# Taking the last two reciprocals of a layer normalisation on GpSimd, as powers of -1, instead of on VectorE

## Chip, cores, metric

One core of one Trainium2 chip. The metric is device time in microseconds (us) of one execution; a run's verdict is "same" when the ratio lies within 2%. Kernels are compared only within the same rounds.

## The reference

```python
# x: float32 [32, 512, 1024], eps = 1e-5
mean = np.mean(x, axis=-1, keepdims=True)
var = np.var(x, axis=-1, keepdims=True)
return ((x - mean) / np.sqrt(var + eps)).astype(np.float32)
```

16384 rows of 1024 values: 67.1 MB in and 67.1 MB out.

## The kernel before

Rows are taken in groups of 128 (one per partition). A tile is eight groups (4 MB); the last two tiles, numbers 15 and 16, have six and two. A ring of six slots in SBUF holds the tiles, and the outputs overwrite the inputs in place. Per tile: SyncE loads; VectorE computes statistics of each half row; GpSimd combines the halves into the negated mean and the sum of squares; ScalarE takes the root; VectorE the reciprocal; GpSimd the product -mean/std; ScalarE writes the normalised rows and issues the store.

```python
TILES = (8,) * 15 + (6, 2)
# ... VectorE, per tile t of K groups that starts in slot `at`
    for k in range(K):
        for s in range(NSUB):
            i = nc.vector.bn_stats(out=stats[:, at + k, s, :], in_=...)   # first one waits for landed[t]
    i.then_inc(taken, 1)
    nc.vector.reciprocal(
        out=rstd[:, at : at + K], in_=std[:, at : at + K]
    )._wait_ge(rooted[t], turn).then_inc(inverse, 1)
# ... GpSimd, per tile: nine small instructions from `taken` to ss, then
    ready.append(gp(g.tensor_mul(out=nmr[...], in0=nm, in1=rstd[...]), inverse, t + 1))
# ... ScalarE, per tile
    nc.scalar.activation(out=std[...], in_=ss[...], func=AF.Sqrt, ...)._wait_ge(*summed[t]).then_inc(rooted[t], 1)
    for k in range(at, at + K):          # the first one waits for ready[t]
        nc.scalar.activation(out=ring[:, k, :], in_=ring[:, k, :], func=AF.Identity,
                             bias=nmr[:, k : k + 1], scale=rstd[:, k : k + 1]).then_inc(act, 1)
    nc.scalar.dma_start(out=<rows of out>, in_=ring[...])._wait_ge(act, ...).then_inc(stored[t], 16)
```

Of the kernel before, what the change touches and what calls it, by code (L numbers as in the profile page):

```python
# [11 lines left out]
SLOT, SLOTS = 8, 6  # L12

FIRST, TURNS = 3, 2

HALVES, PARTS = (4, 4), (8,)

# [2 lines left out]
def kernel(  # L20
# [6 lines left out]
    nc = tc.nc  # L27
    P = nc.NUM_PARTITIONS
# [12 lines left out]
    ALU = mybir.AluOpType  # L41

    def sbuf(name, shape):
        return ctx.enter_context(nc.sbuf_tensor(name, shape, fdt))


    plan, row = [], 0
    for K in TILES:
# [10 lines left out]
    ss, nmean, std, rstd, nmr = (  # L59
        sbuf(n, [P, SLOT * SLOTS]) for n in ("ss", "nmean", "std", "rstd", "nmr")  # L60
    )
    eps_t = sbuf("eps_t", [P, 1])




    def places(name):
        out = [nc.alloc_semaphore(f"{name}_{t}") for t in range(FIRST + SLOTS)]
        for t in range(len(out), len(plan)):
            looped = t < FIRST + TURNS * SLOTS  # L70
            out.append(out[t - SLOTS] if looped else nc.alloc_semaphore(f"{name}_{t}"))
        return out

    def sixteens(sems, t):
# [4 lines left out]
    landed, rooted, stored = places("landed"), places("rooted"), places("stored")  # L79
    taken, inverse, pool, act = map(  # L80
        nc.alloc_semaphore, ("taken", "inverse", "pool", "act")
    )

    def rows_of(a, row, K):
        return a[row * P : (row + K) * P].rearrange("(p k) d -> p k d", p=P)
# [3 lines left out]
    K, row, at = plan[0]  # L89
    first = 0  # L90
    for n, engine, sem in zip(HALVES, (nc.sync, nc.scalar), (landed[0], later)):
        engine.dma_start(
            out=ring[:, at + first : at + first + n, :],
# [5 lines left out]
    for t, (K, row, at) in list(enumerate(plan))[1:]:  # L99
        gone = sorted({owner[r] for r in range(at, at + K) if r in owner})  # L100
        owner.update((r, t) for r in range(at, at + K))
        for g in gone[:-1]:
            nc.sync.wait_ge(stored[g], sixteens(stored, g))
        dma = nc.sync.dma_start(
            out=ring[:, at : at + K, :], in_=rows_of(x2, row, K)
# [5 lines left out]
    def vector(t, arrived, turn):  # L111
        K, row, at = plan[t]
        for k in range(K):
            for s in range(NSUB):
                i = nc.vector.bn_stats(  # L115
                    out=stats[:, at + k, s, :],
                    in_=ring[:, at + k, s * BN_MAX : (s + 1) * BN_MAX],
                )
                if k == 0 and s == 0:
                    i._wait_ge(landed[t], arrived)  # L120
                if t == 0 and k == HALVES[0] and s == 0:
                    i._wait_ge(later, 16)
        i.then_inc(taken, 1)
        nc.vector.reciprocal(  # L124
            out=rstd[:, at : at + K], in_=std[:, at : at + K]
        )._wait_ge(rooted[t], turn).then_inc(inverse, 1)

    nc.vector.memset(eps_t[:], eps_val)  # L128
    for t in range(FIRST):
        vector(t, 16, 1)  # L130
    turn = nc.vector.alloc_register("turn")
# [2 lines left out]
    with nc.vector.Fori(16, 16 * TURNS + 1, 16) as arrived:  # L134
        for t in range(FIRST, FIRST + SLOTS):
            vector(t, nc.vector.lower_val(arrived), turn)
        nc.vector.reg_add(turn, turn, 1)
    for t in range(FIRST + TURNS * SLOTS, len(plan)):
        vector(t, 16, 1)
# [4 lines left out]
    def gp(i, sem, value):  # L144
        nonlocal npool
        i._wait_ge(sem, value).then_inc(pool, 1)
        npool += 1
        return pool, npool

    g = nc.gpsimd  # L150
    for t, (K, row, at) in enumerate(plan):
        parts = stats[:, at : at + K].rearrange("p g s (h c) -> p g (s h) c", h=2)
        mean4, m2 = parts[:, :, :, 1], parts[:, :, :, 2]
        nm, d, h = nmean[:, at : at + K], dev[:, :K], half[:, :K]
        n = gp(
            g.tensor_tensor(out=h, in0=mean4[:, :, 0:2], in1=mean4[:, :, 2:4], op=ALU.add),  # L156
            taken,
            t + 1,
        )
        n = gp(g.tensor_tensor(out=nm, in0=h[:, :, 0], in1=h[:, :, 1], op=ALU.add), *n)  # L160
        n = gp(
            g.tensor_scalar(out=nm, in0=nm, scalar1=-1.0 / H, scalar2=None, op0=ALU.mult),  # L162
            *n,
        )
        n = gp(
            g.tensor_tensor(  # L166
                out=d, in0=mean4, in1=nm.unsqueeze(2).to_broadcast([P, K, H]), op=ALU.add
            ),
            *n,
        )  # L170
        n = gp(g.tensor_mul(out=d, in0=d, in1=d), *n)  # L171
        n = gp(
            g.tensor_scalar(  # L173
                out=d, in0=d, scalar1=float(D // H), scalar2=None, op0=ALU.mult
            ),
            *n,
        )
        n = gp(g.tensor_tensor(out=d, in0=d, in1=m2, op=ALU.add), *n)  # L178
        n = gp(g.tensor_tensor(out=h, in0=d[:, :, 0:2], in1=d[:, :, 2:4], op=ALU.add), *n)  # L179
        summed.append(  # L180
            gp(
                g.tensor_tensor(  # L182
                    out=ss[:, at : at + K], in0=h[:, :, 0], in1=h[:, :, 1], op=ALU.add
                ),
                *n,
            )
        )
        ready.append(
            gp(
                g.tensor_mul(  # L190
                    out=nmr[:, at : at + K], in0=nm, in1=rstd[:, at : at + K]
                ),
                inverse,
                t + 1,
            )
        )


    for t, (K, row, at) in enumerate(plan):
        nc.scalar.activation(  # L200
            out=std[:, at : at + K],
# [7 lines left out]
        for k in range(at, at + K):  # L209
            i = nc.scalar.activation(  # L210
                out=ring[:, k, :],
# [7 lines left out]
            if k - at + 1 in ends:  # L219
                n = parts[ends.index(k - at + 1)]  # L220
                a = k + 1 - n
                nc.scalar.dma_start(
                    out=rows_of(o2, row, K)[:, a - at : a - at + n, :], in_=ring[:, a : a + n, :]
# [41 lines left out]
```

## Time and profile before

| | before |
|---|---|
| time, median of 3 runs | 317.83 us (317.74 to 318.22) |
| span of the profile | 315.9 us |
| VectorE, ScalarE, GpSimd busy | 156.8, 153.0, 39.3 us |
| DMA | 134.24 MB, 425 GB/s over the span |
| issue of the last two stores | 294.43 and 298.01 us |
| landing of the last two stores | 312.2 and 314.7 us |

The upper rows say that no compute engine is the bound. More than 16 us pass between the last instruction of any compute engine and the last byte on the ground.

### The profile page before, as it was taken

The numbers are of one execution on the slowest core, as the hardware profiler recorded it, in microseconds if no ns is written. First come the engines' busy times: TensorE is split into PE (matmuls) and PEld (weight loads), VectorE is DVE, ScalarE is ACT, GpSimd is POOL, SyncE is SP. The second block draws the span as 40 slices with busy tenths as digits, with TensorE's granted clock in tenths as the row PEclk, the third lists the DMA queues.
The fourth block names the chain that finished last, engine by engine and source line by source line (L and its number), as shares of the span: only waits on it lengthen the run. The fifth ranks groups of instructions, "written<-read, shape, count | busy, mean of one in ns | idle before, by whom it ended". The sixth has DMA issues, their size and how long they took to land.

```text
span 315.9 us, 694 instructions
## 1 busy us (share of the span) xinstructions
DVE 156.8 (50%) x274; ACT 153.0 (48%) x146; POOL 39.3 (12%) x174
## 2 busy tenths in 40 slices
DVE  0296595965190752908438093470925619193000
ACT  1006595865925609165190742908338092476600
POOL 0002202022002020020201102011020200203100
DMA  7999999999999999999999999999999999999996
GB/s 292 438 452 411 452 402 407 457 407 461 403 462 415 448 419 444 419 444 431 431 436 427 444 423 440 423 448 415 452 415 456 419 431 442 435 430 427 427 421 288
DMA packets 5043, 134.24 MB, mean 425 GB/s; under 512 B 560, under 2 KB 560, under 8 KB 560
## 3 DMA queue, kind: packets, MB, share of 16 engines
q10 hardware_dynamic: 2592, 69.21, 51.0%
q1 hardware_dynamic: 2448, 65.01, 47.9%
q14 instruction: 3, 0.02, 0.0%
HBM read 67.11 MB, written 67.11 MB: 425 GB/s over the span
## 4 chain that ended last, share of the span: by engine, by line
DMA 61%; DVE 18%; ACT 9%; POOL 4%; issue 2%; ACTq 0%; DVEq 0%; SPq 0%
DMA ring<-in_x_dram 31%; DMA out_dram<-ring 29%; DVE stats L115 17%; ACT ring L210 9%; ACT std L200 1%; POOL dev L173 1%; POOL dev L178 1%; POOL dev L166 0%; POOL dev L171 0%; POOL nmean L162 0%; POOL half L156 0%; POOL half L179 0%; POOL ss L182 0%; DVE rstd L124 0%; POOL nmean L160 0%
## 5 line engine op out<-in xcount | busy, mean ns | idle before, releaser
L115 DVE BATCH_NORM_STATS2 stats<-ring 128x6 f32<-128x512 f32 x256 | 153.5, 678 | 82.2 <-DMA ring<-in_x_dram 81.6
L210 ACT ACTIVATE ring<-ring,nmr,rstd 128x1024 f32<-128x1024 f32 x128 | 146.6, 1227 | 9.3 <-POOL nmr L190 9.3
L200 ACT ACTIVATE std<-ss,eps_t 128x8 f32<-128x8 f32 (+2 forms) x17 | 5.1, 300 | 134.3 <-POOL ss L182 133.9
L156 POOL TENSOR_TENSOR half<-stats 128x16 f32<-128x16 f32 (+2 forms) x17 | 3.9, 232 | 232.9 <-DVE stats L115 232.9
L124 DVE RECIPROCAL rstd<-std 128x8 f32<-128x8 f32 (+2 forms) x17 | 3.4, 200 | 55.4 <-ACT std L200 55.4
L173 POOL TENSOR_SCALAR dev<-dev 128x32 f32<-128x32 f32 (+2 forms) x17 | 5.0, 293 | 1.5
L190 POOL TENSOR_TENSOR nmr<-nmean,rstd 128x8 f32<-128x8 f32 (+2 forms) x17 | 3.5, 203 | 11.9 <-DVE rstd L124 11.9
L178 POOL TENSOR_TENSOR dev<-dev,stats 128x32 f32<-128x32 f32 (+2 forms) x17 | 4.3, 254 | 1.4
L166 POOL TENSOR_TENSOR dev<-stats,nmean 128x32 f32<-128x32 f32 (+2 forms) x17 | 4.1, 239 | 1.4
L171 POOL TENSOR_TENSOR dev<-dev 128x32 f32<-128x32 f32 (+2 forms) x17 | 4.0, 235 | 1.3
L162 POOL TENSOR_SCALAR nmean<-nmean 128x8 f32<-128x8 f32 (+2 forms) x17 | 4.0, 233 | 1.5
L179 POOL TENSOR_TENSOR half<-dev 128x16 f32<-128x16 f32 (+2 forms) x17 | 3.6, 213 | 1.3
L182 POOL TENSOR_TENSOR ss<-half 128x8 f32<-128x8 f32 (+2 forms) x17 | 3.4, 201 | 1.3
L160 POOL TENSOR_TENSOR nmean<-half 128x8 f32<-128x8 f32 (+2 forms) x17 | 3.4, 200 | 1.3
L200 ACT ACT_TABLE_LOAD x1 | 1.3, 1283 | 1.3 <-SPq L52 1.3
L128 DVE MEMSET eps_t<- 128x1 f32 x1 | 0.1, 59 | 1.0 <-SPq L52 1.0
L246 POOL MEMSET const-float32-0.0<- 128x1 f32 x1 | 0.1, 98 | 0.2 <-issue 0.2
L246 POOL MEMSET const-uint8-127<- 128x1 uint8 x1 | 0.1, 102 | 0.0
L246 POOL MEMSET const-bfloat16-1.0<- 128x1 bf16 x1 | 0.1, 101 | 0.0
L246 POOL MEMSET const-float32-1.0<- 128x1 f32 x1 | 0.1, 98 | 0.0
## 6 DMA issues: line engine op xcount, KB each, us to landing
out_dram<-ring ACTq DMA_DIRECT2D x15, 4096.0 KB, 47.4
ring<-in_x_dram SPq DMA_DIRECT2D x14, 4096.0 KB, 44.3
ring<-in_x_dram SPq DMA_DIRECT2D x1, 3072.0 KB, 42.0
out_dram<-ring ACTq DMA_DIRECT2D x1, 3072.0 KB, 17.8
ring<-in_x_dram ACTq DMA_DIRECT2D x1, 2048.0 KB, 12.4
ring<-in_x_dram SPq DMA_DIRECT2D x1, 2048.0 KB, 12.5
ring<-in_x_dram SPq DMA_DIRECT2D x1, 1024.0 KB, 53.7
out_dram<-ring ACTq DMA_DIRECT2D x1, 1024.0 KB, 16.7
```

Source lines behind the costliest of these rows:

```text
L115: i = nc.vector.bn_stats(out=stats[:, at + k, s, :], in_=ring[:, at + k, s * BN_MAX : (s + 1) * BN_MAX],)
L124: nc.vector.reciprocal(out=rstd[:, at : at + K], in_=std[:, at : at + K])._wait_ge(rooted[t], turn).then_inc(inverse, 1)
L156: g.tensor_tensor(out=h, in0=mean4[:, :, 0:2], in1=mean4[:, :, 2:4], op=ALU.add),
L162: g.tensor_scalar(out=nm, in0=nm, scalar1=-1.0 / H, scalar2=None, op0=ALU.mult),
L166: g.tensor_tensor(out=d, in0=mean4, in1=nm.unsqueeze(2).to_broadcast([P, K, H]), op=ALU.add),
L171: n = gp(g.tensor_mul(out=d, in0=d, in1=d), *n)
L173: g.tensor_scalar(out=d, in0=d, scalar1=float(D // H), scalar2=None, op0=ALU.mult),
L178: n = gp(g.tensor_tensor(out=d, in0=d, in1=m2, op=ALU.add), *n)
L179: n = gp(g.tensor_tensor(out=h, in0=d[:, :, 0:2], in1=d[:, :, 2:4], op=ALU.add), *n)
L190: g.tensor_mul(out=nmr[:, at : at + K], in0=nm, in1=rstd[:, at : at + K]),
L200: nc.scalar.activation(out=std[:, at : at + K], in_=ss[:, at : at + K], func=AF.Sqrt, bias=eps_t[:], scale=1.0 / D,)._wait_ge(*summed[t]). ...
L210: i = nc.scalar.activation(out=ring[:, k, :], in_=ring[:, k, :], func=AF.Identity, bias=nmr[:, k : k + 1], scale=rstd[:, k : k + 1],).then ...
```

## The change

Intent: VectorE's end takes two instructions fewer. In the last two tiles GpSimd takes std to the power of -1 itself; its product then waits for its own power instead of for VectorE.

```diff
+LAST = 2
...
+    power = sbuf("power", [P, SLOT])
...
         i.then_inc(taken, 1)
+        if t >= len(plan) - LAST:
+            return
         nc.vector.reciprocal(
...
     nc.vector.memset(eps_t[:], eps_val)
+    nc.vector.memset(power[:], -1.0)
...
+        if t < len(plan) - LAST:
+            n = inverse, t + 1
+        else:
+            n = gp(
+                g.tensor_tensor(out=rstd[:, at : at + K], in0=std[:, at : at + K],
+                                in1=power[:, :K], op=ALU.pow),
+                rooted[t],
+                1,
+            )
         ready.append(
             gp(
                 g.tensor_mul(
                     out=nmr[:, at : at + K], in0=nm, in1=rstd[:, at : at + K]
                 ),
-                inverse,
-                t + 1,
+                *n,
             )
         )
```

More of the change, by code (lines that the diff above doesn't have):

```diff
@@ L187 @@
         )
+        if t < len(plan) - LAST:
+            n = inverse, t + 1
+        else:
+            n = gp(
+                g.tensor_tensor(
+                    out=rstd[:, at : at + K],
+                    in0=std[:, at : at + K],
+                    in1=power[:, :K],
+                    op=ALU.pow,
+                ),
+                rooted[t],
+                1,
+            )
         ready.append(
```

## The prediction

> **What bounds the kernel now.** I read the page's engine shares first, then the row of slices, then time by stage, then the instructions at the end, and last the landings of the last stores. Shares and slices, from the page:
>
> ```profile
> DVE 156.8 (50%) x274; ACT 153.0 (48%) x146; POOL 39.3 (12%) x174
> ...
> DMA  7999999999999999999999999999999999999996
> ...
> HBM read 67.11 MB, written 67.11 MB: 425 GB/s over the span
> ```
>
> No compute engine is busy for more than half of the 315.9 us span, while the DMA engines are full in every slice but the first and the last. 134.22 MB at the 434 GB/s of the middle stage (60 to 260 us, next view) would take 309.3 us; the rest is start and end. So the bytes set the time. The change touches only the last two tiles (6 and 2 row groups, 3 and 1 MB), so the question is what sets the time at the very end. The busy table by stretches (length, then busy time of each engine, clock, DMA share, GB/s):
>
> ```profile
> 60.00:260.00 200.00, 100.90 (x177) 102.98 (x99) 25.55 (x110) 1.00 1.00 434
> ...
> 288.75:294.43 5.68, 2.47 (x4) 5.64 (x5) 1.87 (x9) 1.00 1.02 438
> 294.43:298.01 3.58, 0.17 (x1) 2.67 (x3) 0.19 (x1) 1.00 1.02 439
> 298.01:304.00 5.99, 0.00 (x0) 0.00 (x0) 0.00 (x0) 1.00 0.97 418
> 304.00:314.00 10.00, 0.00 (x0) 0.00 (x0) 0.00 (x0) 1.00 0.92 395
> 314.00:315.90 1.90, 0.00 (x0) 0.00 (x0) 0.00 (x0) 1.00 0.00 0
> ```
>
> The compute engines are finished at 298 us, yet DMA goes on at nearly full rate until about 314: it works off stores already issued. The instructions concerned, from the timeline of the last 60 us (start, duration, instruction, in brackets the idle time before it):
>
> ```profile
> 286.66 0.30 ACT L200 ACTIVATE std<-ss,eps_t 128x6 f32<-128x6 f32 x1 [4.49 <-POOL ss L182]
> 286.99 0.19 DVE L124 RECIPROCAL rstd<-std 128x6 f32<-128x6 f32 x1 [3.16 <-ACT std L200]
> 287.26 0.20 POOL L190 TENSOR_TENSOR nmr<-nmean,rstd 128x6 f32<-128x6 f32 x1 [0.64 <-DVE rstd L124]
> 287.50 6.90 ACT L210 ACTIVATE ring<-ring,nmr,rstd 128x1024 f32<-128x1024 f32 x6 [0.54 <-POOL nmr L190]
> 288.75 2.47 DVE L115 BATCH_NORM_STATS2 stats<-ring 128x6 f32<-128x512 f32 x4 [1.57 <-DMA ring<-in_x_dram]
> ...
> 294.43 0.34 ACTq L222 DMA_DIRECT2D out_dram<-ring  x1
> 294.81 0.29 ACT L200 ACTIVATE std<-ss,eps_t 128x2 f32<-128x2 f32 x1 [0.42 <-ACT ring L210]
> 295.14 0.17 DVE L124 RECIPROCAL rstd<-std 128x2 f32<-128x2 f32 x1 [3.91 <-ACT std L200]
> 295.38 0.19 POOL L190 TENSOR_TENSOR nmr<-nmean,rstd 128x2 f32<-128x2 f32 x1 [1.56 <-DVE rstd L124]
> 295.61 2.37 ACT L210 ACTIVATE ring<-ring,nmr,rstd 128x1024 f32<-128x1024 f32 x2 [0.51 <-POOL nmr L190]
> 298.01 0.34 ACTq L222 DMA_DIRECT2D out_dram<-ring  x1
> ```
>
> Tile 15 (six groups) is handed to the store queue at 294.43, tile 16 (two groups) at 298.01. The times from issue to landing of the last three stores, asked one by one (issued at 282.20, 294.43, 298.01; size, then us to landing):
>
> ```profile
> out_dram<-ring ACTq DMA_DIRECT2D x1, 4096.0 KB, 22.8
> ...
> out_dram<-ring ACTq DMA_DIRECT2D x1, 3072.0 KB, 17.8
> ...
> out_dram<-ring ACTq DMA_DIRECT2D x1, 1024.0 KB, 16.7
> ```
>
> Issue plus landing time: tile 14's store is down at 305.0, tile 15's at 312.2, tile 16's at 314.7. The distances are 7.2 us for 3.15 MB (437 GB/s) and 2.5 us for 1.05 MB (419 GB/s): each store starts moving when the one in front is done. So tile 15's store lies 305.0 - 294.43 = 10.6 us in the queue before its turn, and tile 16's 312.2 - 298.01 = 14.2 us. That is the slack at the end. The chain of waits at the top level does run through these small instructions, but it stops at 298.0 and does not count the standing queue, so its shares mislead here.
>
> **What the Trainium skill says.** "DMA: Bandwidth & Descriptors", section Queues, rings and completion order, says that an engine consumes a ring's descriptors in ring order; the back-to-back landings above agree. The same page, section Bandwidth, puts the fabric ceiling at 435 GB/s; the 434 of the middle stage agrees, so there is no bandwidth left to win. "GPSIMD Engine Reference", section 3.1, gives about 2.6 cycles per element for two-input elementwise work on top of a fixed dispatch: the trace has 205 ns for 128x4 and 234 ns for 128x16 (the same add of strided halves), which is 2.4 ns or 2.9 cycles of the page's 1.2 GHz per element, a near match. Its section 2.1 says that the first call to a freshly loaded library kernel pays about 6 us; no trace here shows it, and I don't know whether a power needs it, so I carry it as the worst case. No page that I found prices the power itself.
>
> **The change part by part.** *Removed:* two reciprocals on VectorE, 0.19 and 0.17 us. VectorE gains nothing from it: after tile 15's reciprocal (over at 287.18) it waits for data until 288.75, and after tile 16's it has no work at all. *Added at the start:* one memset of 128x8 on VectorE, about 0.06 us like the one there now, at 1.06 us; the first data come at 13.48, so it costs nothing. *Moved:* the inverse to GpSimd. Today the stretch from the end of the square root (286.96) to the first output activation (287.50) is 0.54 us: 0.03 to VectorE, 0.19 reciprocal, 0.08 to GpSimd, 0.20 product, 0.04 to ScalarE. In its place come ScalarE to GpSimd, for which I take the 0.08 of VectorE to GpSimd (estimate), the power x, 0.09 to the next GpSimd instruction (as between the others of the row), 0.20, 0.04: 0.41 + x. The handover thus changes by x - 0.13 us. An ordinary GpSimd operation of this size takes 0.19 to 0.20, so even a power as cheap as an add would make each handover 0.07 longer, not shorter. A power in software should be dearer; my guess, with no row to support it, is x = 0.7 for both, with 0.2 to 2 likely. Tile 15's store then goes out 0.57 us later (295.0), and tile 16's, which has both delays in series because ScalarE takes its square root after tile 15's outputs, 1.14 later (299.2). Both are inside the slack of 10.6 and 14.2 us. **Sum on the end: 0.0 us.** With the 6 us added once to tile 15's power, its store goes out at about 301, still 4 us before its turn; tile 16's at about 305.2, 7 us before its turn.
>
> **Rivals.** (1) *The end is bound by the compute chain and the saved hop shows.* For: the dependency chain ends in exactly these instructions. Against: DMA is full for 14 us behind the last instruction; at most two hops would be gained, and the sum above says they are not. It would make at best 317.5. (2) *The power is so slow that the queue runs dry.* It takes a delay beyond 10.6 us less the start of a transfer (about 2 us, estimate from the first load's small rate in slice one and the 0.34 us issue), so over 8 us for six columns, or over some 12 us for both together. Nothing in the profile is near that: the dearest GpSimd instruction is 0.30 us. With 10 us each, tile 16's store would be handed over near 318 and land near 322, giving about 325. (3) *The later stores change how reads and writes interleave.* The last load is in by 288.75, before any of the changed handovers, so no load waits for them and no later buffer is freed by them. No effect. (4) *Program size shifts something earlier.* Two instructions fewer and a memset more on VectorE, two more on GpSimd; VectorE stands idle 82.2 us for data, which swallows it.
>
> **How range and chances follow.** The centre is the time before, 317.8. The three executions before spread over 0.48 us; another build may place its packets a little differently, so I give about twice that on both sides: 317.1 to 318.6. Two per cent is 6.4 us: faster by that is out of reach of 0.4 us of removed work, and I leave 0.01 for it; slower by that needs rival 2 with around 10 us or more per power, for which I leave 0.02.
>
> **What would show it.** The changed profile should show VectorE with 273 instructions and GpSimd with 176; DMA full to about 314; two power rows on GpSimd near 287 and 295; the output activations of tile 15 starting at 287.4 + x; last landing again near 314.7, with the last two times to landing shorter by just what the issues moved (17.8 to about 17.2, 16.7 to about 15.6). The step fails if DMA share falls between 300 and 312 us, or if the last landing moves with the last issue. The prediction fails if a power takes over about 8 us, or if the activations somewhere earlier move.

## The result, and the profile after

| | before | after |
|---|---|---|
| time, median of 6 runs each | 317.87 us (317.74 to 318.22) | 318.25 us (318.03 to 318.91) |
| ratio | | 1.0012, 95% interval 0.9999 to 1.0025: same |
| profiled run: span | 315.9 us | 315.8 us |
| issue of tiles 15 and 16 | 294.43, 298.01 us | 295.77, 299.96 us |
| landing of tiles 15 and 16 | 312.2, 314.7 us | 312.3, 314.8 us |

A ratio here is the mean time of one kernel's fast runs over that of the other's of the same rounds, so it is not quite the ratio of the medians quoted beside it.

Shares and slices on the page after, which answer to the first fence of the prediction:

```profile
DVE 156.4 (50%) x273; ACT 153.0 (48%) x146; POOL 41.7 (13%) x176
...
DMA  7999999999999999999999999999999999999996
...
HBM read 67.11 MB, written 67.11 MB: 425 GB/s over the span
```

VectorE lost 0.4 us, GpSimd gained 2.4, and the DMA row is the same digit for digit. The timeline at the end (start, duration, instruction, idle before):

```profile
286.79 0.30 ACT L218 ACTIVATE std<-ss,eps_t 128x6 f32<-128x6 f32 x1 [4.50 <-POOL ss L188]
287.17 1.35 POOL L198 TENSOR_TENSOR rstd<-std,power 128x6 f32<-128x6 f32 x1 [0.41 <-ACT std L218]
288.60 0.21 POOL L209 TENSOR_TENSOR nmr<-nmean,rstd 128x6 f32<-128x6 f32 x1
288.84 6.90 ACT L228 ACTIVATE ring<-ring,nmr,rstd 128x1024 f32<-128x1024 f32 x6 [1.75 <-POOL nmr L209]
288.88 2.47 DVE L118 BATCH_NORM_STATS2 stats<-ring 128x6 f32<-128x512 f32 x4 [4.93 <-DMA ring<-in_x_dram]
...
296.52 0.73 POOL L198 TENSOR_TENSOR rstd<-std,power 128x2 f32<-128x2 f32 x1 [2.55 <-ACT std L218]
297.33 0.20 POOL L209 TENSOR_TENSOR nmr<-nmean,rstd 128x2 f32<-128x2 f32 x1
297.56 2.37 ACT L228 ACTIVATE ring<-ring,nmr,rstd 128x1024 f32<-128x1024 f32 x2 [1.12 <-POOL nmr L209]
299.96 0.34 ACTq L240 DMA_DIRECT2D out_dram<-ring  x1
```

The idle time in the two output rows is the whole handover, from root to outputs. It was 0.54 and 0.51 us and is now 1.75 and 1.12. So the path through these instructions became 1.21 + 0.61 = 1.8 us longer, not shorter. VectorE's free time does nothing: its statistics of tile 16 start when the data land, at 288.88 us (288.75 before), after an idle 4.93 us; in the kernel before, the reciprocal split the same wait into 3.16 and 1.57 us.

The times from issue to landing of the last two stores:

```profile
out_dram<-ring ACTq DMA_DIRECT2D x1, 3072.0 KB, 16.5
out_dram<-ring ACTq DMA_DIRECT2D x1, 1024.0 KB, 14.8
```

They were 17.8 and 16.7. The stores went out 1.34 and 1.95 us later and were under way 1.3 and 1.9 us less; they landed where they had landed before. (0.12 us of the later issue is no part of the change: tile 14's store, with VectorE's reciprocal in both kernels, was already 0.12 later in this profile.) That is how a standing queue looks: a later issue takes its delay off its own waiting time.

### The profile page after: what moved, and what is told of

Its sections match the earlier page's. It is cut to its first block, busy times and chain, and to the rows that moved or that the text cites. A ratio compares the mean times of both kernels' runs of the same rounds, so it can differ in the third digit from the quotient of the medians.

```text
span 315.8 us, 695 instructions
## 1 busy us (share of the span) xinstructions
DVE 156.4 (50%) x273; ACT 153.0 (48%) x146; POOL 41.7 (13%) x176
## 4 chain that ended last, share of the span: by engine, by line
DMA 61%; DVE 18%; ACT 9%; POOL 5%; issue 2%; ACTq 0%; DVEq 0%; SPq 0%
DMA ring<-in_x_dram 31%; DMA out_dram<-ring 29%; DVE stats L118 17%; ACT ring L228 9%; ACT std L218 1%; POOL rstd L198 1%; POOL dev L179 1%; POOL dev L184 1%; POOL dev L172 0%; POOL dev L177 0%; POOL nmean L168 0%; POOL half L162 0%; POOL half L185 0%; POOL nmean L166 0%; POOL ss L188 0%
## 5 line engine op out<-in xcount | busy, mean ns | idle before, releaser
L228 ACT ACTIVATE ring<-ring,nmr,rstd 128x1024 f32<-128x1024 f32 x128 | 146.6, 1226 | 11.2 <-POOL nmr L209 11.2
L129 DVE RECIPROCAL rstd<-std 128x8 f32<-128x8 f32 x15 | 3.0, 203 | 48.5 <-ACT std L218 48.5
L198 POOL TENSOR_TENSOR rstd<-std,power 128x6 f32<-128x6 f32 (+1 forms) x2 | 2.1, 1041 | 3.0 <-ACT std L218 3.0
```

What stands on the lines that cost most here:

```text
L198: g.tensor_tensor(out=rstd[:, at : at + K], in0=std[:, at : at + K], in1=power[:, :K], op=ALU.pow,),
L228: i = nc.scalar.activation(out=ring[:, k, :], in_=ring[:, k, :], func=AF.Identity, bias=nmr[:, k : k + 1], scale=rstd[:, k : k + 1],).then ...
```

## The experiments

Theory 1: the store queue that stands behind the last instructions hides the longer handover. Theory 2: a later handover costs a little for each us, and 1.0012 is that. Theory 3: the rebuilt program (one more memset, other instruction addresses) costs it.

**The change once more, and its parts.** Four kernels, five rounds each. The changed kernel unaltered:

> The changed kernel once more, to see whether its 1.0012 is real. Theory 1 (the standing store queue hides everything): ratio 0.999 to 1.0015, its interval touching 1.0, the last landing at 314.8 us as before. Theory 2 (the later handover costs a little of the tail): ratio 1.001 to 1.002 again with an interval clear of 1.0, and the last landing later by some 0.4 us. Theory 3 (the rebuilt program's layout, not the powers, costs it): also 1.001 to 1.002, but shown by the memset-only kernel too.

Measured: 318.13 us (318.03 to 318.39), ratio 1.0009, interval 0.9996 to 1.0023; last landing 299.76 + 15.0 = 314.8 us. The lean is smaller than before (1.0012) and still not clear of 1.0; the last landing isn't the 0.4 us later that theory 2 asked for.

Only the memset:

```diff
 # kernel before
     nc.vector.memset(eps_t[:], eps_val)
+    nc.vector.memset(power[:], -1.0)
```

> The kernel before with only the 128x8 memset added at VectorE's start; reciprocals stay on VectorE. Theory 1: ratio 0.999 to 1.001. Theory 2: 1.000, as the handovers of the last two tiles stay at about 294.5 and 298.1 us. Theory 3 (layout): about 1.001 like the changed kernel.

Measured: 317.9 us, ratio 0.9999 (0.9985 to 1.0012). The memset explains nothing that these runs can see; of theory 3 only the rest of the changed kernel's own program remains (taken up under what stays open).

No inverse at all in the last two tiles. Its output is wrong, which doesn't matter for the time. (The comparison with the reference still passed, because rows of 1024 normal draws have a standard deviation close to 1; that pass says nothing.)

```diff
 # changed kernel, last two tiles
-    n = gp(g.tensor_tensor(out=rstd[...], in0=std[...], in1=power[...], op=ALU.pow), rooted[t], 1)
-    ... g.tensor_mul(out=nmr[...], in0=nm, in1=rstd[...])
-    ... scale=rstd[:, k : k + 1]
+    n = rooted[t], 1
+    ... g.tensor_mul(out=nmr[...], in0=nm, in1=std[...])
+    ... scale=std[:, k : k + 1]
```

> Wrong result on purpose in the last two tiles: neither reciprocal nor power; the outputs are scaled by the standard deviation itself. The most that any move of the two reciprocals could win. Handover of each tile shorter than in the kernel before by about 0.2 us (0.54 to 0.32 us: 0.08 + 0.20 + 0.04), last issue at about 297.6 instead of 298.0. Theory 1: ratio 0.999 to 1.001, last landing still 314.7, last time to landing longer by what the issue came earlier. A rival by which the compute chain sets the end: 0.4 us less, ratio 0.9987.

Measured: 317.87 us, ratio 1.0001 (0.9988 to 1.0015). The first output row of tile 15 in its timeline:

```profile
287.17 6.90 ACT L219 ACTIVATE ring<-ring,nmr,std 128x1024 f32<-128x1024 f32 x6 [0.32 <-POOL nmr L200]
```

The handover fell to 0.32 us as expected, the last issue came at 297.48, and that store was under way 17.4 us: landed at 314.9. So even an inverse that costs nothing gains nothing that these runs can see. Since this is the most that any choice of engine for these two inverses could win, the change had nothing to gain here.

All 17 inverses as powers:

```diff
-LAST = 2
+LAST = 17
...
-                rooted[t],
-                1,
+                rooted[t],
+                sixteens(rooted, t) // 16,   # the second use of a looped semaphore waits for 2
```

> All 17 inverses as powers on GpSimd. From the two rows of the changed kernel (0.73 us for 2 columns, 1.35 for 6: 0.42 + 0.155 each) a power of 8 columns should take 1.66 us, each handover 1.5 us longer, GpSimd busy 39.3 + 15 x 1.66 + 2.1 = 66 us (21%). Theory 1: the middle has the queue to hide it too, but tile 0's store comes 1.5 us later when no store is queued, while loads still fill the engines: ratio 1.000 to 1.002. Rival: each store's delay delays the buffer's return and the next load: up to 2 rounds of the ring times 1.5 us, ratio 1.01. If GpSimd and VectorE disturb each other[...], statistics (678 ns each) become longer where a power runs beside them.

Measured: 318.35 us, ratio 1.0014 (1.0000 to 1.0028). Two groups of its profile by form:

```profile
L118 DVE BATCH_NORM_STATS2 stats<-ring 128x6 f32<-128x512 f32 x256 | 153.5, 678 | 134.9 <-DMA ring<-in_x_dram 134.8
...
L198 POOL TENSOR_TENSOR rstd<-std,power 128x8 f32<-128x8 f32 x15 | 25.0, 1666 | 18.0 <-ACT std L218 18.0
```

A power of 8 columns takes 1.67 us, as worked out from the two rows of the changed kernel. With fifteen of them more than in the change the ratio stays far below the 1.01 of the rival; delays do not add up round the ring. The statistics still take 678 ns, so nothing is seen of a disturbance between GpSimd and VectorE. No power of the 17, the first included, took longer than 1.67 us, so the worst case that the prediction carried did not occur in the profiled execution. Whether an earlier execution had paid for it, this profile can't say.

**The dose.** The same power of tile 15 repeated, each into the same place, so that the result stays right; N in all. This delays that store on purpose.

```diff
 # changed kernel, tile 15 only, after its power
+            for _ in range(AGAIN if t == len(plan) - LAST else 0):   # AGAIN = N - 1
+                n = gp(g.tensor_tensor(out=rstd[...], in0=std[...], in1=power[...], op=ALU.pow), *n)
```

> Tile 15's power four times over (the result is the same): tile 15's store is issued at 295.77 + 3 x 1.43 = 300.1 us, 4.9 us before the store in front is down (305.0). Theory 1 (slack): ratio 1.000 to 1.002, last landing 314.8. Theory 2 (a later handover costs in proportion, some 0.2 us for each us): 1.2 us more, ratio 1.004.

> Six powers on tile 15: issue at 295.77 + 5 x 1.43 = 302.9 us, 2.1 us before the store in front is down. Theory 1: still 1.000 to 1.003 if a transfer starts within 2 us of its issue; an excess over the kernel before of d us says the start takes 2.1 + d. Theory 2: 1.6 us more, 1.006.

> Eight powers on tile 15: issue at 305.8 us, 0.8 us after the store in front is down. Theory 1: the queue runs dry; with a start of 2 us the engines stand idle 2.8 us and the last landing is at 317.5, ratio 1.009 (1.006 to 1.011). Theory 2: 2.3 us more, 1.008, without an idle gap in the DMA share.

> Twelve powers on tile 15: issue at 311.5 us. Theory 1: from where the queue is dry, each further us of delay is one us of time: 5.7 us more than with eight, last landing near 323.2, ratio 1.027. Theory 2 (a constant price for each us): 3.5 us more than before, 1.012.

The issue and landing columns are from the profiled runs; medians and ratios from the timed ones, where the kernel before had a median of 317.98 us:

| powers on tile 15 | issue of tile 15 | later than before (294.43) | last landing | median | ratio (95%) |
|---|---|---|---|---|---|
| 4 | 299.34 | 4.9 | 314.8 | 318.20 | 1.0003 (0.9987 to 1.0020) |
| 6 | 302.72 | 8.3 | 315.1 | 318.34 | 1.0006 (0.9990 to 1.0023) |
| 8 | 305.63 | 11.2 | 316.8 | 320.04 | 1.0067 (1.0050 to 1.0084) |
| 12 | 310.83 | 16.4 | 322.2 | 325.39 | 1.0239 (1.0222 to 1.0256) |

This is a kink, not a slope. Theory 2 asked for 1.004 and 1.006 with four and six powers, above both intervals, and for 1.012 with twelve, far below; it falls. (With eight its 1.008 lies inside the interval; there the idle gap below speaks against it.) Theory 1 held, but it put the last landing 0.7 us too late with eight powers (317.5 expected, 316.8 measured) and 1.0 too late with twelve (323.2 and 322.2): a repeated power took 1.40 us and not 1.43, and a store starts sooner than the 2 us assumed. From eight to twelve powers the issue moves by 5.2 us and the time by 5.35: each us is paid in full. Read back, 11.2 us of delay cost 2.06 (320.04 - 317.98) and 16.4 cost 7.41, so about the first 9.1 and 9.0 us were free. That is the slack; the change used 1.3 of it.

The busy table by stretches shows the queue run dry. With six powers:

```profile
302.00:304.00 2.00, 0.00 (x0) 0.98 (x2) 0.53 (x1) 1.00 1.00 430
304.00:306.00 2.00, 0.00 (x0) 1.49 (x2) 0.40 (x2) 1.00 0.95 406
```

With eight:

```profile
302.00:304.00 2.00, 0.00 (x0) 2.00 (x3) 0.00 (x0) 1.00 0.65 279
304.00:306.00 2.00, 0.00 (x0) 1.60 (x2) 0.00 (x0) 1.00 0.00 0
306.00:308.00 2.00, 0.00 (x0) 0.87 (x2) 0.92 (x2) 1.00 0.93 393
```

The last two columns are DMA share and GB/s. With six powers the engines go on without a gap; with eight they run dry. Finer stretches of the run with eight:

```profile
303.00:303.25 0.25, 0.00 (x0) 0.25 (x2) 0.00 (x0) 1.00 0.61 262
...
306.00:306.25 0.25, 0.00 (x0) 0.23 (x1) 0.00 (x0) 1.00 0.00 0
306.25:306.50 0.25, 0.00 (x0) 0.06 (x1) 0.11 (x1) 1.00 1.14 492
306.50:306.75 0.25, 0.00 (x0) 0.00 (x0) 0.25 (x1) 1.00 2.52 1081
```

A share of 2.52 can't be a busy time: the view counts each packet whole in the stretch in which it starts. So the end of the bytes must be read from the packets themselves, in the packet records of the trace. Tile 14's packets of 32 KB took 1.2 us each; all but one had started by 303.15 and the last started at 303.77, so the 16 engines ran out one after the other between 303.5 and 305.0 us. The new store's first packet started at 306.48, 0.85 us after its issue at 305.63. (With twelve powers it is 0.84: issue 310.83, first packet 311.67.)

**A wide last tile.** Here I meant to expose the end in another way: one last tile of eight groups in place of six and two, once with the reciprocal and once with the power on that last tile.

```diff
-TILES = (8,) * 15 + (6, 2)
+TILES = (8,) * 16            # both kernels
...
-LAST = 2
+LAST = 1                     # the kernel with the power only
```

> The kernel before with a last tile of eight groups instead of six and two, so that the end is exposed: the last load is in at about 288.8 us, statistics take 9.6, sums and root some 3.5, the outputs 9.2, so its 4 MB store is issued at about 311, when the queue has been dry since about 303; start 2 us, 9.8 us to move: last landing at 323, ratio 1.025 (1.02 to 1.035). DMA share should fall to near 0 between 304 and 312.

> The same tiling with the last tile's inverse as a power on GpSimd. Now nothing hides the handover: a power of 8 columns is 1.66 us, handover 0.41 + 1.66 = 2.07 instead of 0.54: 1.5 us longer than wide_before, ratio to the kernel before higher by 0.0048. If GpSimd's route were as good as VectorE's where it matters, or better, the two would be equal or this one faster by up to 0.1 us.

Measured: 317.76 us, ratio 0.9998 (0.9984 to 1.0011), and 317.52 us, ratio 0.9993 (0.9980 to 1.0007). My expectation was wrong by 8 us for the first and, with its 1.5 us more, by 10 for the second. It took the arrival of the last load, 288.8 us, over from the kernel before; the wide tile's load was in at 279.5. The first lines below are what the two DMA queues moved from 277 to 288 us in the kernel before (q1 carries SyncE's loads, q10 here the stores; packets, MB, share):

```profile
q10 hardware_dynamic: 132, 3.80, 80.1%
q1 hardware_dynamic: 128, 0.93, 20.1%
```

And from 262 to 279 us in the kernel with the wide tile and the reciprocal:

```profile
q10 hardware_dynamic: 130, 3.74, 50.9%
q1 hardware_dynamic: 125, 3.60, 49.1%
```

Both queues move about equally many packets. A load of two groups has small ones (0.93 MB in 128) against 28.8 KB each of the store, so it gets a fifth of the bandwidth, and its 1 MB takes about 12 us. The wide load gets half. So in the wide kernel the last store was issued at 302.0 us, still before the queue was dry, and with the power at 303.4, just at its edge. The pair shows the handover (0.55 and 2.07 us, as expected) but not its price. I had not tested the expectation against the queue shares, and a look at them would have told. The expected 0.0048 between the two kernels did not appear, since the end was not exposed.

**The handover where nothing hides it.** So the end was exposed by an idle stretch on GpSimd ahead of tile 15's sums, the same in both kernels:

```diff
+        n = taken, t + 1
+        for _ in range(8 if t == len(plan) - 2 else 0):
+            n = gp(g.tensor_tensor(out=idle[:], in0=power[:], in1=power[:], op=ALU.pow), *n)
         n = gp(
             g.tensor_tensor(out=h, in0=mean4[:, :, 0:2], in1=mean4[:, :, 2:4], op=ALU.add),
-            taken,
-            t + 1,
+            *n,
         )
```

> Reciprocals on VectorE as before, with eight idle powers of 8 columns on GpSimd ahead of tile 15's sums (8 x 1.75 = 14.0 us), so that tile 15's store is issued at 294.4 + 14.0 = 308.4 us, after the queue has run dry at about 303.3. With eight powers in a row the issue at 305.6 landed 2.1 us later than before; this one is 2.8 us later still: 4.9 us more than the kernel before, ratio 1.0155 (1.014 to 1.017).

> The same eight idle powers, and the last two inverses as powers on GpSimd as in the change. Theory (the change only makes the handover longer, by x - 0.13 = 1.22 us for tile 15 where the power takes 1.35, and that is hidden by the queue in the real kernel): here nothing hides it, so 1.2 us more than late_before, ratio 1.0194. Rival (with two instructions fewer on VectorE the end is at least as quick): equal to late_before or less.

Measured: 322.76 us, ratio 1.0155 (1.0141 to 1.0169), with the reciprocal; 323.92 us, ratio 1.0194 (1.0180 to 1.0208), with the power. Both ratios are the expected ones, and the intervals do not overlap, though by the 2% rule the verdicts read "same" and "unclear". Tile 15's first output row with the reciprocal:

```profile
300.48 6.89 ACT L219 ACTIVATE ring<-ring,nmr,rstd 128x1024 f32<-128x1024 f32 x6 [0.54 <-POOL nmr L199]
```

and with the power:

```profile
302.38 6.89 ACT L235 ACTIVATE ring<-ring,nmr,rstd 128x1024 f32<-128x1024 f32 x6 [1.75 <-POOL nmr L216]
```

The medians differ by 1.16 us (the means of the spans by 1.28), the handovers by 1.21. The two rows lie 1.90 us apart because the profiled run with the reciprocal was the fastest of its five (321.8 us); tile 14's store was already 0.67 us earlier in it (281.44 against 282.11). Where the end is bound by this path, the move of the inverse to GpSimd costs, within the noise, what it adds to tile 15's handover. The 0.61 us more of tile 16 stay hidden even here: with the power its store was issued at 313.49 us and tile 15's was down only at 318.0.

## Why the prediction was right

**The bound** was right: DMA sets the time and has the same digits after. No inverse at all moved nothing (ratio 1.0001). That no bandwidth was left to win rests on the ceiling cited in the prediction; no run here tried it.

**The handover, 0.41 + x,** was right in its fixed part: with the measured powers it gives 1.76 and 1.14 us, against 1.75 and 1.12. The hop from ScalarE to GpSimd, which I had to estimate, took the 0.08 I had taken (root over at 287.09, power at 287.17).

**The size of x** was mis-sized for tile 15. I guessed 0.7 for both powers, without a row to support it; they took 1.35 for 6 columns and 0.73 for 2. I had not let x grow with the columns. Tile 15's store therefore went out 1.34 us later instead of 0.57, tile 16's 1.95 instead of 1.14 (0.12 of each is tile 14's). It did not matter, because both are far inside the slack. Two sums of the prediction are also slightly off: tile 16's handover was 0.51 us and not 0.54, so with x = 0.7 its store would go out 1.17 us later, not 1.14; and the range of 317.1 to 318.6 is one and a half times the spread of 0.48 on each side, not twice.

**The slack** was right in sum, and partly by luck: I called the queue dry at the landing of tile 14's store, 305.0 us, and allowed 2 us for a start, over 8 us net. The dose gives 9.0 to 9.1. The packet records of the kernel before show its engines done with that store's bytes between 303.5 and 304.5 us, so the last one 0.5 before the landing is reported, and a new store moves its first packet 0.85 after its issue, not 2. The two errors lean opposite ways. With the measured sizes, 304.5 - 0.85 - 294.43 gives 9.2.

**The rivals.** That the saved hop shows (1): there is no saved hop, the handover grew by 1.21 and 0.61 us. That the queue runs dry (2): it needs some 9 us, which a single power is far from. That reads and writes interleave otherwise (3): tile 16's load was in at 288.88 against 288.75, and the delay of tile 14's store (0.12 us) is of the same size before any changed instruction. Program size (4): the memset alone is 0.9999; the rest was not tested by itself, and the idle time of VectorE can't swallow what the next paragraph shows, since that lies outside the span.

**What stays open:** the changed kernel stood at 1.0012 and 1.0009, and all powers at 1.0014, each with an interval that begins at or just below 1.0. The record says where this lean lies, because it lists each run's span (first to last instruction) beside its time. In the second run the spans average 315.98 us for the changed kernel and 316.14 for the kernel before: no longer. What differs is the rest, time less span: 2.19 to 2.26 us in all eleven runs of the changed kernel and 1.77 to 1.87 in the nine of the kernel before. With all powers it is 2.15 to 2.25, but with four to twelve powers on tile 15 it is 1.76 to 1.86, as in the kernel before. So the lean of about 0.4 us is outside the span and comes from neither the powers nor the handover; it goes with the build of the program, and what in the build sets it was not tested. That the measured 318.25 lies 0.4 us above the prediction's centre is therefore nothing that the prediction had in its sum; the range covered it by its width. No version here beats the kernel before clear of noise.

## What to carry to other kernels

In a kernel that DMA bounds, ask of each end-of-kernel instruction when its store's turn in the queue comes, not when the last instruction ends: issue time plus time to landing of the last three stores gives a first figure of the slack (here 10.6 us), from which the start of a transfer and the delay of the landing's report go off; the 9 us that were left here hid everything. Moving a small operation to a less busy engine saves time only if the operation lies on the path that ends last and the other engine does not take longer over it: here the trip through VectorE was 0.54 us and GpSimd's own way 1.75. To learn what a hidden step costs, expose it with a known delay in both versions and compare.

## What the Trainium skill lacked or had wrong

- "GPSIMD Engine Reference" (section 3.1 has only adds): it has no price for a power. Here one of 2, 6 and 8 columns on 128 partitions took 0.73, 1.35 and 1.67 us, that is 0.42 us and some 0.155 for each column, against 0.19 to 0.21 for a product of 2 or 6 columns in all.
- "DMA: Bandwidth & Descriptors", section Queues, rings and completion order: it says that the engines change between queues packet by packet, and leaves out what follows for the sharing of bandwidth. Here two queues with about as many packets each (132 and 128) moved 3.80 and 0.93 MB in the same stretch, and a load of 1 MB took about 12 us beside a store of larger packets.
